# Sixteen slots of h at multiples of 256 bytes, and the shifted half of a weight buffer in one of its turns out of four

## The chip, the core and the metric

The kernel runs on one core of a Trainium2 chip. The metric is device time in microseconds (us) of one execution. The median of three runs of the kernel before is 1770.55 us (1770.16 to 1771.66).

## What is computed

One macaron block of a Conformer: a half-step SwiGLU feed-forward, a token mixer (attention heads beside multi-scale pooling groups), a second half-step feed-forward, and a final RMSNorm. Each of the three normalised inputs is scaled and shifted by numbers that depend on a conditioning vector `c`. Cut to what matters here:

```python
mod = silu(c) @ w_ada + b_ada                         # 9 sections of 2048, "ada" below
h = modulate(rmsnorm(x, g1), sh1, sc1)
x = x + 0.5 * gate1 * swiglu(h, ffn1_w_in, ffn1_w_out)
h = modulate(rmsnorm(x, g2), sh2, sc2)
x = x + gate2 * mixer(h, w_in, ..., w_out)
h = modulate(rmsnorm(x, g3), sh3, sc3)
x = x + 0.5 * gate3 * swiglu(h, ffn2_w_in, ffn2_w_out)
return rmsnorm(x, final_norm_g)
```

There are 256 tokens, 2048 channels and 5504 hidden channels, all in float32.

## The kernel before

**Arithmetic.** Each float32 operand of the large products is split into a high part, rounded to the TensorE type `fp32r`, and a low part, the remainder. A product takes three matmuls, high by high, low by high and high by low (`mm3`, L242, L243, L244). So a 128x128 weight tile costs three matmuls, each with 256 moving columns (the tokens) and one weight load.

**Weights.** The weights come in 614 pieces of eight tiles (128x1024 float32, 512 KB), in the order in which TensorE will use them. `next_piece` brings a piece into use and at the same time starts work for the next ones: ScalarE casts a piece to `wh` in two halves (L193), VectorE subtracts to make `wl` in two halves (L203), and SyncE's queue loads a raw piece (L185). Four `wh` buffers and three `wl` buffers go round in turn (`part_tile`), and five raw buffers. Beside this run 144 loads of `ada` (1 MB each), each with a multiplication on VectorE (L112) that yields 128 numbers of `mod`; they are spread over the pieces at fixed rates, so how many there are for each piece doesn't depend on how fast anything runs.

**Activations.** The moving operand of the products is one of: `h` (L242 to L244, 16 tiles per normalised input, tag `h`, 16 slots), `hraw` (the same slots, 258 columns, made before the root of the norm is known), `g` and `mix` (tag `pair`, 43 slots of 2048 bytes), and in the q, k and v projections (`project`, L768) the weights themselves, where `h` is the stationary operand. Each tile of these holds the high part and behind it the low part.

**Addresses.** They decide this change; all here are bytes within a partition, in the built program. The slots of `h` begin at 29440, which is a multiple of 256. A slot is as long as the largest tile of its tag, `hraw` with 2 x 272 columns, which is 2176 bytes, eight and a half times 256. So slots 0, 2, 4, ... begin at a multiple of 256, and slots 1, 3, 5, ... 128 past one. In the first feed-forward the tiles of channel blocks 0 to 15 lie in slots 1 to 8, 11, 10, 15, 14, 13, 9, 12 and 0, so that blocks 0 to 11 alternate between the two, 12 and 13 lie 128 past a multiple, and 14 and 15 at one. The high and the low part are 1024 bytes apart in `h` and in `g`. All 43 slots of `g` and `mix` begin at multiples of 256. A small tile (`gap`, 16 columns) puts all `wh` buffers, two `wl` buffers and the raw buffers 64 past a multiple of 256, and the last `wl` buffer lies 192 past one. The fourth `wh` buffer is 32 columns longer (`BEHIND`), and its second half begins 16 columns, 64 bytes, later than it otherwise would, so that these four weight tiles lie 128 past a multiple of 256. Below, 64, 128 and 192 stand for these distances, and 0 for a multiple of 256.

```python
GAP = 16
BEHIND = {"wh": (0, 0, 0, 2 * GAP), "wl": (0, 0, 0)}
```

Of the kernel before, what the change touches and what calls it, by code (L numbers as in the profile page):

```python
# [10 lines left out]
F32 = mybir.dt.float32  # L11
F32R = mybir.dt.float32r
# [4 lines left out]
P = 128  # L17
SEQ = 256
# [5 lines left out]
HD = 128  # L24
UT = 8
UN = UT * P
# [21 lines left out]
NEG = -3.0e38  # L48
GAP = 16
BEHIND = {"wh": (0, 0, 0, 2 * GAP), "wl": (0, 0, 0)}  # L50
WARM = 9
QSCALE = float(HD) ** -0.5

# [12 lines left out]
def block_kernel(ctx, tc, order, xT, cvec, wada, wts, wf, vecs, out):  # L66
# [105 lines left out]
    HALF = UN // 2  # L172

    def part_tile(kind):

        behind = BEHIND[kind]
        i = turns[kind] % len(behind)
        turns[kind] += 1
        w = wpool.tile([P, UN + behind[i]], F32R, tag=f"{kind}{i}", name=kind, bufs=1)
        return w[:, :HALF], w[:, HALF + behind[i] // 2 : UN + behind[i] // 2]  # L180

    def load_piece():
        if state["loaded"] < wts.shape[0]:
# [76 lines left out]
    class Stats:  # L260
# [6 lines left out]
        def add(self, d):  # L267
            t = {}

            def square():  # L270
                t["sq"] = work.tile([P, SEQ], F32, tag="act", name="sq", bufs=3)
                nc.scalar.activation(t["sq"], x[d], AF.Square)

            def total():
                if d == KD - 1:
                    self.last = t["sq"]
                elif self.acc is None:
                    self.acc = work.tile([P, SEQ], F32, tag="gf", name="acc", bufs=3)
                    nc.vector.tensor_copy(out=self.acc, in_=t["sq"])
                else:  # L280
                    nc.vector.tensor_add(out=self.acc, in0=self.acc, in1=t["sq"])

            later(square, total)
            if d == KD - 1:
                step_chains(0)

        def rms_row(self, meanwhile=None, between=None):

            st = sm_tile()
            parts = self.parts or (self.acc, self.last)  # L290
            for i, part in enumerate(parts):
                nc.tensor.matmul(st[:, :SEQ], lhsT=ones, rhs=part, start=i == 0, stop=i == len(parts) - 1)  # L292
            self.row = work.tile([P, SEQ], F32, tag="rrow", name="rrow", bufs=1)
            guess, rest = (work.tile([P, SEQ], F32, tag="hu", name=n, bufs=3) for n in ("guess", "rest"))
            first, newton = inverse_root(self.row, st[:, :SEQ], D, guess, rest)
            first()
            if between:
                between()
            newton()
            if meanwhile:  # L300
                meanwhile()
            return self.row

    def make_h(d, rrow, a_col, b_col):

        u = work.tile([P, SEQ], F32, tag="hu", name="hu", bufs=3)
        nc.vector.scalar_tensor_tensor(out=u, in0=x[d], scalar=a_col, in1=rrow, op0=ALU.mult, op1=ALU.mult)
        h = big.tile([P, 2, SEQ], F32R, tag="h", name="h", bufs=16)

        def high():  # L310
            nc.scalar.activation(h[:, 0, :], u, AF.Identity, bias=b_col)  # L311

        def low():
            nc.vector.scalar_tensor_tensor(  # L314
                out=h[:, 1, :], in0=u, scalar=b_col, in1=h[:, 0, :].bitcast(F32), op0=ALU.add, op1=ALU.subtract
            )

        return h, high, low

    def make_raw(d, a_col, b_col):  # L320

        h = big.tile([P, 2, SEQ + 16], F32R, tag="h", name="hraw", bufs=16)[:, :, : SEQ + 2]
        b2 = b_col.to_broadcast([P, 2])

        def high():
            nc.scalar.activation(h[:, 0, :SEQ], x[d], AF.Copy, scale=a_col)
            nc.scalar.copy(out=h[:, 0, SEQ:], in_=b2)

        def low():
            nc.vector.scalar_tensor_tensor(  # L330
                out=h[:, 1, :SEQ], in0=x[d], scalar=a_col, in1=h[:, 0, :SEQ].bitcast(F32),
                op0=ALU.mult, op1=ALU.subtract,
            )
            nc.vector.tensor_sub(out=h[:, 1, SEQ:], in0=b2, in1=h[:, 0, SEQ:].bitcast(F32))

        return h, high, low
# [40 lines left out]
    def swiglu(ab, j, g):  # L377

        t = {}

        def act():
            t["s"] = work.tile([P, SEQ], F32, tag="act", name="silu", bufs=3)
            nc.scalar.activation(t["s"], ab[:, :SEQ], AF.Silu)

        def product():
            t["g"] = work.tile([P, SEQ], F32, tag="gf", name="gf", bufs=3)
            nc.vector.tensor_mul(out=t["g"], in0=ab[:, SEQ:512], in1=t["s"])
            g[j] = pair_tile([P, 2, SEQ], F32R, f"g{j}")

        def high():  # L390
            nc.scalar.copy(out=g[j][:, 0, :], in_=t["g"])

        def low():
            nc.vector.tensor_sub(out=g[j][:, 1, :], in0=t["g"], in1=g[j][:, 0, :].bitcast(F32))

        return act, product, high, low
# [377 lines left out]
    def norm_heads(pts, name):  # L774
# [4 lines left out]
        def squares(tt):  # L779
            nc.scalar.copy(out=qr[tt], in_=pts[tt].rearrange("p (a b) -> p a b", a=4))  # L780
            for i in range(4):
                junk = work.tile([P, HD], F32, tag="act", name="junk", bufs=3)
                nc.scalar.activation(
                    junk, qr[tt][:, i, :], AF.Square, accum_out=ss[:, tt * 4 + i : tt * 4 + i + 1]
                )
# [309 lines left out]
```

## Time and profile before

| | |
|---|---|
| median of the runs | 1770.55 us |
| the profiled execution: its time, its span | 1770.31 us, 1768.6 us |
| TensorE matmul busy | 1753.8 us (99%), 14,966 matmuls |
| TensorE granted clock | 0.998 of full speed |
| VectorE busy | 1371.4 us (78%) |
| ScalarE busy | 922.2 us (52%) |
| DMA, mean over the span | 272 GB/s |

A busy share says little of TensorE, since the records of matmuls that follow each other overlap: one takes 277 to 280 ns in the record, but the next starts some 115 ns after it. What counts is the distance between starts, which the timeline gives, and the number of matmuls in a window. Times in the views are counted from the start of the span.

### The profile page before, as it was taken

The page shows a single profiled execution, that of the slowest core. Times are in us where ns is not written, and L with a number is a line of the kernel's source. Part 1 is how long each engine was busy: PE and PEld are TensorE (multiplying, and loading weights), DVE is VectorE, ACT ScalarE, POOL GpSimd, SP SyncE. Part 2 cuts the span into 40 slices and gives each one's busy share as a digit, 9 for nine tenths or more (in the row PEclk, how much of TensorE's full clock was granted, in tenths as well). Part 3 has the DMA queues.
Part 4 walks back from the last instruction along what each step waited for, and adds up shares of the span by engine and source line. Part 5 has one row for each costly group of instructions (what it writes and reads, how often), then busy time and mean ns, then how long its engine had stood idle before and what let it go on. Part 6 is the DMA issues. An engine that isn't in the chain of part 4 may idle for free.

```text
span 1768.6 us, 37313 instructions
## 1 busy us (share of the span) xinstructions
PE 1753.8 (99%) x14966; PEld 1743.8 (99%) x14966; DVE 1371.4 (78%) x2390; ACT 922.2 (52%) x1871; POOL 8.3 (0%) x54
## 2 busy tenths in 40 slices
PE   9999999999999999999999999999999999999997
PEld 7999999999999999999999999999999999999997
DVE  7899889999988888797989998777765555555554
ACT  7644445555554444477766555544444444544442
POOL 0000000000000000100000000000000000000000
PEclk9999999999999999999999999999999999999999
DMA  9889898888889989767966977877775555555553
GB/s 367 317 319 331 319 339 316 309 308 314 311 319 335 328 329 334 286 237 301 344 223 248 330 285 249 296 268 259 262 258 189 189 188 191 191 191 192 194 195 112
DMA packets 111937, 480.79 MB, mean 272 GB/s; under 512 B 12425, under 2 KB 12689, under 8 KB 93329
## 3 DMA queue, kind: packets, MB, share of 16 engines
q1 hardware_dynamic: 111762, 478.39, 75.4%
q8 instruction: 117, 1.92, 0.4%
q14 instruction: 58, 0.48, 0.1%
HBM read 476.24 MB, written 2.11 MB: 270 GB/s over the span
## 4 chain that ended last, share of the span: by engine, by line
PE 98%; ACT 1%; DMA 1%; DVE 0%; issue 0%; SPq 0%; DVEq 0%
PE mm L243 30%; PE mm L242 29%; PE mm L244 29%; PE mm L768 8%; DMA ada<-in_wada 1%; ACT wh L193 0%; ACT spill L454 0%; DVE y L1029 0%; PE sm L802 0%; PE sm L832 0%; PE sm L881 0%; PE sm L872 0%; PE sm L292 0%; PE sm L699 0%; PE sm L701 0%
## 5 line engine op out<-in xcount | busy, mean ns | idle before, releaser
L193 ACT CAST wh<-raw 128x512 fp32r<-128x512 f32 x1228 | 701.2, 620 | 725.1 <-PE mm L243 442.0
L203 DVE TENSOR_TENSOR wl<-raw,wh 128x512 fp32r<-128x512 f32 x1228 | 788.2, 686 | 319.0 <-issue 285.2
L242 PE MATMUL mm<-h,wh 128*128 128x256 f32 x2800 | 782.1, 279 | 0.8 <-ACT h L311 0.4
L243 PE MATMUL mm<-h,wh 128*128 128x256 f32 x2800 | 782.8, 280 | 0.1
L244 PE MATMUL mm<-h,wl 128*128 128x256 f32 x2800 | 781.9, 279 | 0.0
L242 PEld LDWEIGHTS mm<-h,wh 128*128 128x128 f32 x2800 | 526.3, 188 | 2.0 <-ACT spill L454 1.0
L243 PEld LDWEIGHTS mm<-h,wh 128*128 128x128 f32 x2800 | 525.8, 188 | 0.4 <-DVE h L314 0.3
L244 PEld LDWEIGHTS mm<-h,wl 128*128 128x128 f32 x2800 | 526.0, 188 | 0.0
L244 PE MATMUL mm<-g,wl 128*128 128x256 f32 x1376 | 380.8, 277 | 0.0
L243 PE MATMUL mm<-g,wh 128*128 128x256 f32 x1376 | 380.5, 277 | 0.0
L242 PE MATMUL mm<-g,wh 128*128 128x256 f32 x1376 | 380.5, 276 | 0.0
L112 DVE SCALAR_TENSOR_TENSOR ada<-ada,crow 128x2048 f32<-128x2048 f32 x144 | 329.2, 2286 | 23.5 <-DMA ada<-in_wada 22.9
L243 PEld LDWEIGHTS mm<-g,wh 128*128 128x128 f32 x1376 | 258.4, 188 | 0.0
L244 PEld LDWEIGHTS mm<-g,wl 128*128 128x128 f32 x1376 | 258.4, 188 | 0.0
L242 PEld LDWEIGHTS mm<-g,wh 128*128 128x128 f32 x1376 | 258.3, 188 | 0.0
L768 PE MATMUL mm<-wh,h 128*128 128x256 f32 x768 | 137.3, 282 | 0.0
L768 PEld LDWEIGHTS mm<-wh,h 128*128 128x128 f32 x768 | 117.4, 188 | 0.5 <-issue 0.2
L768 PE MATMUL mm<-wl,h 128*128 128x256 f32 x384 | 107.2, 279 | 0.0
L768 PEld LDWEIGHTS mm<-wl,h 128*128 128x128 f32 x384 | 72.3, 188 | 0.0
L244 PE MATMUL mm<-mix,wl 128*128 128x256 f32 x256 | 70.9, 277 | 0.0
L243 PE MATMUL mm<-mix,wh 128*128 128x256 f32 x256 | 70.8, 277 | 0.0
L242 PE MATMUL mm<-mix,wh 128*128 128x256 f32 x256 | 70.8, 277 | 0.0
(166 smaller groups left out, 1002.9 us busy)
## 6 DMA issues: line engine op xcount, KB each, us to landing
raw<-in_wts SPq DMA_DIRECT2D x614, 512.0 KB, 4.4
ada<-in_wada SPq DMA_DIRECT2D x144, 1024.0 KB, 7.6
x<-in_xT SPq DMA_DIRECT2D x4, 512.0 KB, 5.5
out<-y SPq DMA_DIRECT2D x8, 256.0 KB, 2.2
fb<-frow_d SPq DMA_DIRECT2D x4, 256.0 KB, 8.0
vec<-in_vecs SPq DMA_DIRECT2D x1, 109.5 KB, 10.1
wfc<-in_wf SPq DMA_DIRECT2D x1, 64.0 KB, 5.7
crow<-in_cvec SPq DMA_DIRECT2D x1, 8.0 KB
```

The costliest lines, as they stand in the source:

```text
L112: nc.vector.scalar_tensor_tensor(out=r, in0=r, scalar=1.0, in1=crow, op0=ALU.mult, op1=ALU.mult, accum_out=mod[section][:, t : t + 1],)
L193: nc.scalar.copy(out=wh[i], in_=raws[0][:, i * HALF : (i + 1) * HALF])
L203: nc.vector.tensor_sub(out=wl[i], in0=raw[:, i * HALF : (i + 1) * HALF], in1=wh[i].bitcast(F32))
L242: nc.tensor.matmul(out_ap, lhsT=wh, rhs=hk[:, 0, :], start=start, stop=False, skip_group_check=shared)
L243: nc.tensor.matmul(out_ap, lhsT=wh, rhs=hk[:, 1, :], start=False, stop=False, skip_group_check=shared)
L244: nc.tensor.matmul(out_ap, lhsT=wl, rhs=hk[:, 0, :], start=False, stop=stop, skip_group_check=shared)
L768: nc.tensor.matmul(pts[tt][:, c], lhsT=lhs, rhs=rhs[:, c], start=k == 0 and not half and not i, stop=k == KD - 1 and i == 2, skip_group_ch ...
```

## The change

Four edits. `h` and `hraw` get slots of 576 columns (2304 bytes, nine times 256), so that all 16 slots begin at a multiple of 256; the two parts of `h` stay 1024 bytes apart, and the low part of `hraw` moves to 1152 bytes behind the high one (from 1088). The second half of the fourth `wh` buffer is shifted only where the turn of that buffer is 1 modulo 4; in its other turns it lies 64 past a multiple of 256, like every other `wh` half. To pay for the 2048 bytes, the tags `hu` and `act` get two buffers in place of three. The rest of the tiles move up by 2048 bytes, so their distances from multiples of 256 stay as they were.

```diff
+SLOT = 576
...
         behind = BEHIND[kind]
         i = turns[kind] % len(behind)
+        turn = turns[kind] // len(behind)
         turns[kind] += 1
         w = wpool.tile([P, UN + behind[i]], F32R, tag=f"{kind}{i}", name=kind, bufs=1)
-        return w[:, :HALF], w[:, HALF + behind[i] // 2 : UN + behind[i] // 2]
+        at = HALF + (behind[i] // 2 if turn % 4 == 1 else 0)
+        return w[:, :HALF], w[:, at : at + HALF]
...
-                t["sq"] = work.tile([P, SEQ], F32, tag="act", name="sq", bufs=3)
+                t["sq"] = work.tile([P, SEQ], F32, tag="act", name="sq", bufs=2)
...
-            guess, rest = (work.tile([P, SEQ], F32, tag="hu", name=n, bufs=3) for n in ("guess", "rest"))
+            guess, rest = (work.tile([P, SEQ], F32, tag="hu", name=n, bufs=2) for n in ("guess", "rest"))
...
+    def h_slot(name, half):
+
+        return big.tile([P, SLOT], F32R, tag="h", name=name, bufs=16)[:, : 2 * half].rearrange("p (a b) -> p a b", a=2)
+
...
-        u = work.tile([P, SEQ], F32, tag="hu", name="hu", bufs=3)
+        u = work.tile([P, SEQ], F32, tag="hu", name="hu", bufs=2)
...
-        h = big.tile([P, 2, SEQ], F32R, tag="h", name="h", bufs=16)
+        h = h_slot("h", SEQ)
...
-        h = big.tile([P, 2, SEQ + 16], F32R, tag="h", name="hraw", bufs=16)[:, :, : SEQ + 2]
+        h = h_slot("hraw", SEQ + P // 4)[:, :, : SEQ + 2]
...
-            t["s"] = work.tile([P, SEQ], F32, tag="act", name="silu", bufs=3)
+            t["s"] = work.tile([P, SEQ], F32, tag="act", name="silu", bufs=2)
...
-                junk = work.tile([P, HD], F32, tag="act", name="junk", bufs=3)
+                junk = work.tile([P, HD], F32, tag="act", name="junk", bufs=2)
```

On every engine the instructions stand in the same order before and after. On TensorE these rows of before stand 293 us into the span, in the first feed-forward; `h_2883` and `h_3061` are the tiles of blocks 14 and 15 (slots 12 and 0), `h_977` and `h_1165` those of blocks 4 and 5 (slots 5 and 6), and `wh_3693` and `wl_3735` lie at 64.

```order
L242 MATMUL mm_3799<-h_2883,wh_3693 128x256
L243 MATMUL mm_3799<-h_2883,wh_3693 128x256
L244 MATMUL mm_3799<-h_2883,wl_3735 128x256
L242 MATMUL mm_3799<-h_3061,wh_3693 128x256
L243 MATMUL mm_3799<-h_3061,wh_3693 128x256
L244 MATMUL mm_3799<-h_3061,wl_3735 128x256
L242 MATMUL mm_3828<-h_977,wh_3693 128x256
L243 MATMUL mm_3828<-h_977,wh_3693 128x256
L244 MATMUL mm_3828<-h_977,wl_3735 128x256
L242 MATMUL mm_3828<-h_1165,wh_3693 128x256
L243 MATMUL mm_3828<-h_1165,wh_3693 128x256
L244 MATMUL mm_3828<-h_1165,wl_3735 128x256
```

The same rows stand there after the change, and only the slots differ: `h_977`, 128 past a multiple of 256 before, now begins at one.

On VectorE the only rows that differ carry a wait. Here stand the first tiles of the mixer's h (`hu` is the product of x, scale and norm, from which `h` is made); before:

```order
L307 SCALAR_TENSOR_TENSOR hu_9847<-x0_74,a4_103,rrow_9777 128x256
L307 SCALAR_TENSOR_TENSOR hu_9860<-x0_74,a4_103,rrow_9777 128x256
L314 SCALAR_TENSOR_TENSOR h_9849<-hu_9847,b4_106,h_9849 128x256 [waits Activation_49]
L307 SCALAR_TENSOR_TENSOR hu_9871<-x0_74,a4_103,rrow_9777 128x256
L314 SCALAR_TENSOR_TENSOR h_9862<-hu_9860,b4_106,h_9862 128x256 [waits Activation_49]
```

and after:

```order
L314 SCALAR_TENSOR_TENSOR hu_9847<-x0_74,a4_103,rrow_9777 128x256
L314 SCALAR_TENSOR_TENSOR hu_9860<-x0_74,a4_103,rrow_9777 128x256
L321 SCALAR_TENSOR_TENSOR h_9849<-hu_9847,b4_106,h_9849 128x256 [waits Activation_49]
L314 SCALAR_TENSOR_TENSOR hu_9871<-x0_74,a4_103,rrow_9777 128x256 [waits DVE_49]
L321 SCALAR_TENSOR_TENSOR h_9862<-hu_9860,b4_106,h_9862 128x256 [waits Activation_49]
```

Nothing moved; the third `hu` now waits for VectorE's own earlier instruction, since it takes the buffer of the first. Four rows of VectorE and 28 of ScalarE differ in this way, each by a wait of an engine for itself, and none on the other engines.

## Rows read from the trace of the kernel before

**Rows 1.** The page: busy time by engine, and the chain that ended last.

```profile
PE 1753.8 (99%) x14966; PEld 1743.8 (99%) x14966; DVE 1371.4 (78%) x2390; ACT 922.2 (52%) x1871; POOL 8.3 (0%) x54
PE 98%; ACT 1%; DMA 1%; DVE 0%; issue 0%; SPq 0%; DVEq 0%
```

**Rows 2.** Windows of five stages: PE, PEld, DVE, ACT, POOL busy, clock, DMA.

```profile
40.00:500.00 460.00, 460.00 (x3931) 460.00 (x3931) 421.12 (x693) 232.11 (x446) 0.00 (x0) 1.00 0.89 319
505.00:739.00 234.00, 234.00 (x2055) 234.00 (x2055) 196.87 (x337) 113.38 (x223) 6.94 (x42) 1.00 0.91 331
752.00:905.00 153.00, 153.00 (x1297) 151.81 (x1297) 133.74 (x255) 110.97 (x288) 0.34 (x3) 1.00 0.79 292
1060.00:1520.00 460.00, 460.00 (x3939) 460.00 (x3939) 300.82 (x496) 223.97 (x434) 0.00 (x0) 1.00 0.66 233
1522.00:1740.00 218.00, 218.00 (x1915) 218.00 (x1915) 116.48 (x205) 104.36 (x192) 0.00 (x0) 1.00 0.57 193
```

**Rows 3.** Timeline of PE, first feed-forward: start us, duration us, instruction.

```profile
292.77 0.28 PE L242 MATMUL mm<-h,wh 128*128 128x256 f32 x1
...
294.47 0.28 PE L242 MATMUL mm<-h,wh 128*128 128x256 f32 x1
...
296.57 0.28 PE L242 MATMUL mm<-h,wh 128*128 128x256 f32 x1
```

**Rows 4.** The same view, first matmuls of the first output product.

```profile
504.70 0.28 PE L244 MATMUL mm<-g,wl 128*128 128x256 f32 x1
...
507.52 0.28 PE L244 MATMUL mm<-g,wl 128*128 128x256 f32 x1
...
507.88 0.28 PE L244 MATMUL mm<-g,wl 128*128 128x256 f32 x1
...
508.21 0.28 PE L244 MATMUL mm<-g,wl 128*128 128x256 f32 x1
```

**Rows 5.** The same view around one shifted half, in the same product.

```profile
590.34 0.28 PE L242 MATMUL mm<-g,wh 128*128 128x256 f32 x1
...
590.69 0.28 PE L242 MATMUL mm<-g,wh 128*128 128x256 f32 x1
...
592.11 0.28 PE L242 MATMUL mm<-g,wh 128*128 128x256 f32 x1
```

**Rows 6.** Groups by line and form: count, busy us, mean ns, idle before.

```profile
L242 PE MATMUL mm<-h,wh 128*128 128x256 f32 x2800 | 782.1, 279 | 0.8 <-ACT h L311 0.4 <-ACT spill L454 0.3
L242 PE MATMUL mm<-g,wh 128*128 128x256 f32 x1376 | 380.5, 276 | 0.0
L242 PE MATMUL mm<-mix,wh 128*128 128x256 f32 x256 | 70.8, 277 | 0.0
```

**Rows 7.** Timeline of PE in the projections, two stretches.

```profile
753.70 0.39 PE L768 MATMUL mm<-wh,h 128*128 128x256 f32 x2
...
755.06 0.39 PE L768 MATMUL mm<-wh,h 128*128 128x256 f32 x2
...
759.32 0.40 PE L768 MATMUL mm<-wh,h 128*128 128x256 f32 x2
...
760.73 0.28 PE L768 MATMUL mm<-wh,h 128*128 128x256 f32 x1
```

**Rows 8.** Waits from 184 to 244 us: us in total, times, longest.

```profile
DVE ada L112 <- DMA ada<-in_wada: 6.8, 5, 2.2
```

**Rows 9.** The window of the same stretch, columns as in rows 2.

```profile
184.00:244.00 60.00, 60.00 (x514) 60.00 (x513) 54.70 (x95) 26.91 (x49) 0.00 (x0) 1.00 0.90 331
```

**Rows 10.** Timeline of DVE, subtractions at two places (starts 0.60 us apart).

```profile
177.58 2.49 DVE L203 TENSOR_TENSOR wl<-raw,wh 128x512 fp32r<-128x512 f32 x4
...
228.28 1.88 DVE L203 TENSOR_TENSOR wl<-raw,wh 128x512 fp32r<-128x512 f32 x3
```

**Rows 11.** Timeline of PE, the first matmuls that read these.

```profile
184.34 0.28 PE L244 MATMUL mm<-h,wl 128*128 128x256 f32 x1
...
229.43 0.28 PE L244 MATMUL mm<-h,wl 128*128 128x256 f32 x1
```

## Prediction

> **What bounds the kernel now.** The page first: TensorE is busy 99% of the span, and 98% of the chain that ended last is PE [rows 1]. The kernel is thus as long as its 14,966 matmuls are apart, plus a few us at both ends, as long as nothing comes late. A duration says nothing here, so next the windows, for matmuls per stage [rows 2]. A window counts those that reach over its edges as well, some 2.4 more than start in it (0.28 us over 0.117). In the first feed-forward's input product, with h as moving operand, that is 460 us / 3,929 = 117.1 ns from start to start, in the second's 460 / 3,937 = 116.9; in the output products, with g, 234 / 2,053 = 114.0 and 218 / 1,913 = 114.0. The reader should see that this does not follow the load on the other engines: VectorE is busy 92% of the window at 40 us, 65% in that at 1060 us and 84% in that at 505 us, and DMA 0.89, 0.66 and 0.91, and the two h stages are alike, as are the two of g. The clock is 1.00 in all of them, the upper level (2.4 GHz).
>
> Then the timeline inside a stage of h [rows 3]. From 292.77 to 294.47 us TensorE reads blocks 14 and 15, both at 0: 15 matmuls in 1.70 us, 113.3 ns each. At 294.47 it goes on to block 4, at 128, and alternates from there: 18 matmuls in 2.10 us, 116.7 ns. Same code, same weights at 64, same neighbours. In the g stage, where every moving tile lies at 0, a steady stretch has 113.3 as well, and the three matmuls before 590.69 take 0.35 us; the twelve after it, of a shifted half, take 1.42 us, 118 ns each [rows 5]. So there are two things that cost: a moving operand at 128, and weights at 128.
>
> There is a third, and it is what makes me doubt. The rate has a memory. At the entry from h to g, 24 matmuls from 504.70 to 507.52 take 117.5 ns each, though moving tiles lie at 0 and weights at 64; it ends where the piece of the `wl` buffer at 192 comes, and from 507.88 three matmuls take 0.33 us [rows 4]. In the projections the same pair of distances (h at 0, weights at 64) runs at 113.3 ns from 753.70 and at 117.5 from 759.32, twelve matmuls each [rows 7]. So the slow rate, once entered, can outlast its cause until a distance changes.
>
> **The change, part by part.** The sum is made against the profiled execution's own 1770.3 us, which is 0.2 us under the median.
>
> Slots of h. The h groups of L242, L243 and L244 have 2,800 matmuls each, 8,400 [rows 6]. The first 130 or so belong to the start, where pieces come late. With all slots at 0 the other 8,270 should run as blocks 14 and 15 do now: from 117.0 (the mean of the two h windows) to 113.3, 3.65 ns each, -30.2 us. Both ends: nothing, if they run slow all the time; -30.2 if always as in [rows 3]. I take the fast end, since the nearest case, the g stages, has just these distances throughout and is at 114.0 with its shifted halves included.
>
> Shifted halves that stay. One piece in 16 keeps one, 24 matmuls a piece: 8,270 / 384 = 22 of them among h. One costs twelve times 118 less 113.3, some 0.06 to 0.07 us with the matmul behind it: +1.5 us.
>
> Shifted halves that go, in g and mix. 3 x (1,376 + 256) = 4,896 matmuls [rows 6] are 204 pieces with 51 shifted halves, 13 after: 38 x 0.07 = -2.7 us.
>
> `hraw` and the projections. The 240 matmuls with hraw keep a low part at 128 and gain at most the same 3.65 ns, 0.9 us; I take -0.5. In the 1,152 of L768 h is the stationary operand and the weights move; both rates occur there with h at either distance, so the bounds are all slow and all fast, +1.4 and -3.5 us about what is now a mixture; I take -0.5 for the shifted halves that go.
>
> Two buffers in place of three. The new waits are of VectorE and ScalarE for themselves, 32 in all; one bounds at an instruction's length, under 0.7 us (the `wl` subtraction is the longest of the neighbours, [rows 10]), the other at nothing, since the earlier reader stands ahead in the same queue. What covers them is the lead of `wl` over TensorE, up to 4.9 us (below). Zero.
>
> What comes due next. A faster TensorE asks for pieces sooner, and VectorE is nearly full in the first feed-forward. Look at its lead. The third of the four subtractions from 177.58 ends at 177.58 + 2 x 0.60 + 0.69 = 179.47 and is read at 184.34, 4.87 us ahead. The first of the three from 228.28 ends at 228.97 and is read at 229.43, 0.46 us ahead [rows 10, 11]. In between VectorE worked 54.7 of 60 us and waited 6.8 for ada loads, so it was full [rows 8, 9]. After the change TensorE is 16 pieces x 24 x 3.65 ns = 1.4 us earlier at that point: the lead would be 0.9 below zero, and TensorE waits as long. If loads land no sooner, the five late ada products add up to 3 pieces x 24 x 3.65 ns = 0.26 us each. +2 us, between 0.9 and 5 (a lead as short as this at several other places of the stage, each 1 us more).
>
> Sum: 1770.3 - 30.2 + 1.5 - 2.7 - 0.5 - 0.5 + 2 = 1739.9; I add 0.6 for entries into stages that run slow for up to two pieces (48 x 4.2 ns = 0.2 us each, three of them): 1740.5 us.
>
> A rule speaks against all of this. The Trainium skill's page "SBUF — State Buffer", section "Who interferes with whom", gives TensorE two independent read ports, one for the moving operand and one for the weight load, and says: "PE and ACT never wait on anyone." By it distances in SBUF would be worth nothing and the time stay at 1770.3. [Rows 3] disagree: the one thing that changes at 294.47 is which slots are read.
>
> **The rivals.** *The slow rate sticks* (the other side). If what keeps the pipeline fast today is that it is disturbed every four pieces, then with a disturbance every sixteen and with no change of slot distance it may sit at 117.5. For it: [rows 4, 7]. Against: in g the fast rate holds from one shifted half to the next and through the changes from `wl` at 64 to 192 and back; and the one slow stretch ended at such a change, which comes in every third piece, shifted half or not. Each slow matmul costs 4.2 ns, and there are 8,270 + 4,896 that could be: the gain of 30 us is gone when 7,100 of these 13,170, 54%, run slow, and with all of them slow the time is 1740.5 + 13,170 x 4.2 ns = 1796 us. Partly, with the slow rate held from a disturbance to the next `wl` at 192 in a third of the pieces, it is 1740.5 + 18 = 1759.
>
> *VectorE or DMA becomes the bound.* DMA is at 0.91 and 331 GB/s where it is asked most [rows 2, 9]; TensorE would ask for 3% more, 341 GB/s. If the whole first stage ran as fast as it does now, the change would keep only the second's gain: 3,930 x 3.8 ns = 15 us lost, 1755. Against it: the g stage has the same rates of loads, moves 331 GB/s at 114.0 ns and shows no wait of TensorE; I give it up to 1750.
>
> *The distance is not the cause.* If h is slow for what goes with it (copies to spill tiles, additions), only the shifted halves change: 38 fewer in g and mix and 64 fewer in h, at 0.02 to 0.07 us each, 1764 to 1768. For it there is only the rule above; against it [rows 3], in one stage within 4 us.
>
> **How the numbers follow.** The forecast, 1734 to 1748 us, 0.74. Slow rate in part, 1748 to 1765, 0.09; sticking for most, above 1765, 0.07. First stage bound by VectorE or DMA, 1746 to 1755, 0.06. Distance not the cause, 1764 to 1768, 0.04. The range for 8 in 10 takes in the forecast, with the stalls at their bound, and the half of the partial cases: 1734 to 1756. A measurement of this kernel tells 0.2%, 3.5 us, from no change. Faster by more: the first two, the fourth and a part of the last, 0.90; within it 0.04; slower 0.06.
>
> **What would show it.** Right: the windows at 40 and 1060 us hold 3.0% more matmuls, at 113.5 to 113.8 ns, like those of g; twelve slow matmuls in one piece out of 16; VectorE's share in the first stage rises by 3%, with waits for ada there longer, and TensorE waits for `wl` near 230 us for about 1 us at a time. Wrong: steady stretches of h at 117.5 with weights at 64, above all such that last past a `wl` at 192; or a first feed-forward that is no shorter while the second is.

## The result, and the profile after

The changed kernel takes 1745.68 us (median of 4 runs, 1745.34 to 1746.95), against 1770.40 for the kernel before beside it (1770.16 to 1771.66). The ratio is 0.986 [0.9843, 0.9877], so it is faster by 24.7 us. The profiled execution took 1745.73 us with a span of 1744.0.

The page of the kernel after; its lines answer to [rows 1]:

```profile
PE 1726.4 (99%) x14966; PEld 1714.9 (98%) x14966; DVE 1369.9 (79%) x2390; ACT 923.7 (53%) x1871; POOL 8.3 (0%) x54
PE 95%; DMA 2%; DVE 2%; ACT 1%; issue 0%; SPq 0%; DVEq 0%
```

The counts are the same and TensorE is still the chain, but DMA and VectorE now hold 4% of it, where they had 1%. The windows of the kernel after, columns as in [rows 2] (the one at 505 us now reaches past the end of g, so that g itself is read from the table below):

```profile
40.00:500.00 460.00, 457.24 (x4016) 456.20 (x4016) 427.24 (x706) 239.43 (x456) 0.00 (x0) 1.00 0.91 325
752.00:905.00 153.00, 153.00 (x1287) 151.88 (x1286) 133.13 (x251) 108.98 (x286) 0.45 (x4) 1.00 0.78 286
1060.00:1520.00 460.00, 460.00 (x4056) 460.00 (x4055) 305.43 (x505) 229.49 (x444) 0.00 (x0) 1.00 0.68 237
```

In the second feed-forward the window holds 4,056 matmuls in place of 3,939, so 460 us / 4,053.6 = 113.5 ns each. The first holds 4,016 in place of 3,931, which is 114.6 ns; here TensorE is no longer busy all the time (457.24 of 460). The window over the projections holds 1,287 against 1,297, but it no longer covers the same matmuls, since the stage now starts 11 us earlier (741.7 us in place of 752.3); the table below has the projections themselves. The clock is 1.00 in all three, as before, so none of this is the clock.

The timeline of TensorE in the kernel after, at five places; start, duration, instruction. The first three rows are the same matmuls as in [rows 3], the next two those of [rows 4], then the place in g that was a shifted half, then four of the projections:

```profile
289.60 0.28 PE L245 MATMUL mm<-h,wh 128*128 128x256 f32 x1
...
291.30 0.28 PE L245 MATMUL mm<-h,wh 128*128 128x256 f32 x1
...
293.34 0.28 PE L245 MATMUL mm<-h,wh 128*128 128x256 f32 x1
...
495.15 0.28 PE L247 MATMUL mm<-g,wl 128*128 128x256 f32 x1
...
497.87 0.28 PE L247 MATMUL mm<-g,wl 128*128 128x256 f32 x1
...
580.71 0.28 PE L245 MATMUL mm<-g,wh 128*128 128x256 f32 x1
...
582.07 0.28 PE L245 MATMUL mm<-g,wh 128*128 128x256 f32 x1
...
743.09 0.40 PE L775 MATMUL mm<-wh,h 128*128 128x256 f32 x2
...
744.50 0.40 PE L775 MATMUL mm<-wh,h 128*128 128x256 f32 x2
...
748.78 0.40 PE L775 MATMUL mm<-wh,h 128*128 128x256 f32 x2
...
750.20 0.40 PE L775 MATMUL mm<-wh,h 128*128 128x256 f32 x2
```

From 289.60 to 291.30 the 15 matmuls of blocks 14 and 15 take 1.70 us as before; the 18 behind them, of blocks 4 to 9, now take 2.04 us, 113.3 ns each as well (2.10 before). The entry into g, 24 matmuls from 495.15 to 497.87, takes 113.3 ns each; it was 117.5. At 580.71 the twelve matmuls that were a shifted half in [rows 5], and now lie at 64, take 1.36 us, 113.3 each. In the projections it went the other way: the stretch that ran at 113.3 in [rows 7] takes 1.41 us for twelve, 117.5 each, like the other.

The waits of the kernel after from 40 to 500 us, in total, times and longest:

```profile
DVE ada L113 <- DMA ada<-in_wada: 24.1, 27, 1.9
...
PE mm L247 <- DVE wl L206: 2.8, 5, 0.9
```

and one of the five, in the timeline of TensorE (in brackets the idle time ahead and its releaser):

```profile
212.19 0.28 PE L246 MATMUL mm<-h,wh 128*128 128x256 f32 x1
213.38 0.39 PE L247 MATMUL mm<-h,wl 128*128 128x256 f32 x1 [0.91 <-DVE wl L206]
213.60 0.28 PE L245 MATMUL mm<-h,wh 128*128 128x256 f32 x1
```

VectorE waits 24.1 us for `ada` loads in this stretch, twice the 11.9 of before, and five times TensorE waits for a `wl` that VectorE makes behind such a wait. At 213.38 the matmul starts 1.19 us after the one ahead of it.

The table below adds up the distances from each matmul's start to the next one's, from the traces, by the stage that the matmul belongs to, for this kernel and the experiments. "Of it waits" sums what each distance of over 130 ns in the first feed-forward's h has beyond 130 ns; it is a part of the column ahead. There are 4,128 matmuls with h in the first feed-forward, 4,272 in the second and the mixer, 4,128 with g and 1,152 in the projections.

| us | h, first | of it waits | h, the rest | g | projections |
|---|---|---|---|---|---|
| before | 485.2 | 1.8 | 499.6 | 470.5 | 136.6 |
| after | 475.4 | 6.2 | 485.5 | 468.4 | 137.9 |
| slots alone | 479.6 | 8.4 | 487.4 | 470.4 | 138.2 |
| fewer shifts alone | 485.3 | 3.2 | 498.4 | 468.4 | 135.9 |
| never shifted | 476.4 | 7.8 | 484.9 | 467.8 | 137.7 |
| no distance changes, a short execution | 475.8 | 6.8 | 484.9 | 467.8 | 138.0 |
| the same kernel, a long execution | 488.1 | 1.9 | 484.9 | 477.0 | 138.0 |
| h at 128 | 479.8 | 5.4 | 491.6 | 468.8 | 137.2 |
| h in two groups | 485.9 | 5.3 | 498.8 | 468.7 | 136.8 |
| mixer's h alternates | 475.2 | 6.0 | 486.4 | 468.4 | 137.2 |
| lag of four | 471.0 | 2.0 | 485.4 | 468.4 | 139.2 |
| half product | 471.0 | 2.1 | 485.4 | 468.4 | 137.9 |
| lag of four, never shifted | 470.3 | 2.2 | 484.7 | 467.8 | 139.3 |
| before with two buffers | 488.1 | 4.7 | 499.6 | 470.5 | 137.0 |

### The profile page after: what moved, and what is told of

Its sections match the earlier page's. It is cut to its first block, busy times and chain, and to the rows that moved or that the text cites. A ratio compares the mean times of both kernels' runs of the same rounds, so it can differ in the third digit from the quotient of the medians.

```text
span 1744.0 us, 37330 instructions
## 1 busy us (share of the span) xinstructions
PE 1726.4 (99%) x14966; PEld 1714.9 (98%) x14966; DVE 1369.9 (79%) x2390; ACT 923.7 (53%) x1871; POOL 8.3 (0%) x54
## 4 chain that ended last, share of the span: by engine, by line
PE 95%; DMA 2%; DVE 2%; ACT 1%; issue 0%; SPq 0%; DVEq 0%
PE mm L247 29%; PE mm L245 29%; PE mm L246 28%; PE mm L775 8%; DMA ada<-in_wada 2%; DVE wl L206 1%; DVE ada L113 0%; ACT wh L196 0%; ACT spill L461 0%; DVE y L1036 0%; PE sm L888 0%; PE sm L809 0%; PE sm L839 0%; PE sm L295 0%; PE sm L879 0%
## 5 line engine op out<-in xcount | busy, mean ns | idle before, releaser
L247 PE MATMUL mm<-h,wl 128*128 128x256 f32 x2800 | 774.1, 276 | 2.8 <-DVE wl L206 2.8
L245 PE MATMUL mm<-h,wh 128*128 128x256 f32 x2800 | 774.3, 277 | 0.7 <-ACT spill L461 0.5
L246 PE MATMUL mm<-h,wh 128*128 128x256 f32 x2800 | 773.4, 276 | 0.1
L113 DVE SCALAR_TENSOR_TENSOR ada<-ada,crow 128x2048 f32<-128x2048 f32 x144 | 329.4, 2287 | 48.4 <-DMA ada<-in_wada 47.8
L775 PEld LDWEIGHTS mm<-wh,h 128*128 128x128 f32 x768 | 117.6, 188 | 0.5 <-issue 0.2
```

Source lines behind the costliest of these rows:

```text
L113: nc.vector.scalar_tensor_tensor(out=r, in0=r, scalar=1.0, in1=crow, op0=ALU.mult, op1=ALU.mult, accum_out=mod[section][:, t : t + 1],)
L245: nc.tensor.matmul(out_ap, lhsT=wh, rhs=hk[:, 0, :], start=start, stop=False, skip_group_check=shared)
L246: nc.tensor.matmul(out_ap, lhsT=wh, rhs=hk[:, 1, :], start=False, stop=False, skip_group_check=shared)
L247: nc.tensor.matmul(out_ap, lhsT=wl, rhs=hk[:, 0, :], start=False, stop=stop, skip_group_check=shared)
L775: nc.tensor.matmul(pts[tt][:, c], lhsT=lhs, rhs=rhs[:, c], start=k == 0 and not half and not i, stop=k == KD - 1 and i == 2, skip_group_ch ...
```

## The experiments

The theory of the prediction is that the distances of the operands from multiples of 256 bytes set whether matmuls start 113.3 or about 117.8 ns apart. The rivals are that the slow rate sticks, that something other than h's distance makes h slow, and that VectorE or DMA takes the gain. Diffs are against the changed kernel unless the text says otherwise. Where no range is given, a time is the median of a kernel's runs.

### The two parts, each alone

The slots alone, with the shift in every turn of the fourth `wh` buffer:

```diff
-        at = HALF + (behind[i] // 2 if turn % 4 == 1 else 0)
+        at = HALF + behind[i] // 2
```

> Only the slots of h (and the two buffers that pay for them); the half of the fourth wh buffer is shifted in every turn, as before. If the rate follows from the distances (theory one): steady stretches of h at 113.3 ns, twelve slow matmuls in every fourth piece, 115 more of them at 2.2 ns over 24 matmuls, 0.053 us each, so about 6 us more than the changed kernel, less up to 1.5 us in the projections if the more frequent shift ends slow stretches there: 1750 us. If the slow rate is kept off by the shifts (theory two): 1745 or less.

Measured: 1754.47 us (1751.37 to 1758.27), ratio 0.99 [0.9882, 0.9918].

The shift alone, in the kernel before, with its slots and its three buffers:

```diff
+        turn = turns[kind] // len(behind)
...
-        return w[:, :HALF], w[:, HALF + behind[i] // 2 : UN + behind[i] // 2]
+        at = HALF + (behind[i] // 2 if turn % 4 == 1 else 0)
+        return w[:, :HALF], w[:, at : at + HALF]
```

> Only the shift in one turn of four; slots of h and three buffers as before. Theory one: the g and mix stages lose 38 shifted halves, 2.3 us; h keeps its alternation at 116.7 ns and gains at most 1 us: 1767 to 1769. If the shift and not the slots made the gain: 1750 or less. If a rarer shift lets the slow rate stick: over 1771.

Measured: 1766.58 us (1764.70 to 1766.85), ratio 0.9966 [0.9953, 0.9979].

Beside them the kernel before took 1771.44. So the slots are worth 17.0 us with the shift in every turn, the rarer shift 4.9 us with the old slots, and both together 24.7. By the medians they do more together than apart, though the runs of the slots alone lie up to 6.9 us from each other. The table shows where: h falls by 17.8 us with the slots, by 1.1 with the rarer shift and by 23.9 with both. Of the 6.1 us between the slots alone and both, 2.2 are waits, which the slots alone raise to 8.4 us. Among h tiles that alternate a shifted half more or less changes little (the h of the first feed-forward is the same 485 us with either), while among tiles that all lie at 0 it costs. That the slots alone move 5.6 us of h in the first stage and 12.2 in the rest, with g as before, rules out that something other than the slots' distance makes h slow (the two buffers, which come with the slots, gain nothing by themselves: last experiment).

### Is the shift needed at all?

The fourth `wh` buffer keeps its extra columns, so that the last `wl` buffer stays at 192, but its half is never shifted:

```diff
-        at = HALF + (behind[i] // 2 if turn % 4 == 1 else 0)
+        at = HALF
```

> The changed kernel with no half ever shifted; the last wl buffer stays at 192, so one distance still changes in every third piece. Theory one: 38 shifted halves fewer at 0.053 us, 2 us: 1743.7, with the projections as slow as they are. Theory two (the shift ends slow stretches): slow pieces at 117.7 ns in h or g after the entries into stages, each 0.1 us, and 1746 or more.

Measured: 1745.75 us (1743.55 to 1747.04), ratio 0.985 [0.9834, 0.9866]; the changed kernel has 0.986 [0.9843, 0.9877], so the two can't be told apart. Every column of the table but one gains a little (0.6 us in h of the rest, 0.6 in g, 0.2 in the projections); the first feed-forward is 1.0 us longer, since its waits grow by 1.6.

Then the last distance that changes in the steady stretches, the `wl` buffer at 192, is taken away as well, by 32 columns behind the last `wl` buffer in place of the fourth `wh` buffer. All weights now lie at 64 and all of h and g at 0:

```diff
-BEHIND = {"wh": (0, 0, 0, 2 * GAP), "wl": (0, 0, 0)}
+BEHIND = {"wh": (0, 0, 0, 0), "wl": (0, 0, 2 * GAP)}
...
-        at = HALF + (behind[i] // 2 if turn % 4 == 1 else 0)
+        at = HALF
```

> No half shifted, and the last wl buffer at 64 as well (the 32 columns stand behind it), so that no distance changes within a stage of h or g. Theory one without memory: 1743.7 as without the shift. With the memory that the projections show: the rate with which a stage is entered stays to its end; the second h stage is entered from hraw, at 120 ns, and would stay at 117.7 for its 4,000 matmuls, 17 us more, and the g stage behind it another 8: 1760 to 1770. If the change of wl to 192 costs something itself, less than 1743.

Measured: ten runs in two groups, seven from 1743.91 to 1749.30 and three from 1765.12 to 1768.22. The median is 1746.23 us, the ratio 0.9887 [0.985, 0.9925]; neither says much of two groups. The profiled execution was one of the short ones, and its stages are those of the kernel that is never shifted. So it was run once more, on another chip, to find a long one in a trace:

> The kernel with all wl buffers at 64 and no shift once more, to see where its long executions (three of ten, 20 us over the others) lose the time. If the slow rate is kept through a whole stage, an execution is near 1745, or a stage of h or g runs at 117.8 ns throughout with all clocks and loads as before: near 1766. If the long ones are something else: times between, or slower stretches with late loads.

Measured: eight runs, four from 1742.77 to 1748.81 and four from 1761.94 to 1767.71 (median 1755.37, ratio 0.9902 [0.9858, 0.9946]). The profiled execution took 1766.93. Its windows:

```profile
40.00:500.00 460.00, 460.00 (x3908) 460.00 (x3908) 418.38 (x687) 231.26 (x443) 0.00 (x0) 1.00 0.89 317
505.00:735.00 230.00, 230.00 (x1955) 230.00 (x1954) 191.43 (x327) 108.02 (x212) 0.00 (x0) 1.00 0.89 321
...
1060.00:1520.00 460.00, 460.00 (x4057) 460.00 (x4057) 312.24 (x524) 232.33 (x451) 0.00 (x0) 1.00 0.69 238
```

and the same windows of the short execution of the same kernel:

```profile
40.00:500.00 460.00, 456.96 (x4012) 455.71 (x4012) 427.43 (x707) 237.66 (x457) 0.00 (x0) 1.00 0.90 324
505.00:735.00 230.00, 230.00 (x2025) 229.89 (x2024) 193.25 (x331) 109.43 (x217) 6.94 (x42) 1.00 0.92 331
...
1060.00:1520.00 460.00, 460.00 (x4061) 460.00 (x4060) 306.12 (x505) 230.02 (x445) 0.00 (x0) 1.00 0.68 237
```

In the long one the first feed-forward runs at 460 / 3,905.6 = 117.8 ns, through h and g alike, with TensorE busy all the time: of its 258 pieces all but the second and the third have 117.6 to 118.0 ns. From the mixer on both run at 113.3. The clock is 1.00 in both, TensorE waits less in the long one, and no address differs. So the same operands at the same distances have two rates, and a run can stay in the slow one for 700 us when nothing disturbs it.

One thing that changes the rate can be seen in the short execution: a wait of TensorE can do it, with no distance changed. Here are the rows at two waits for `wl` in its first feed-forward, with every weight at 64 and every tile of h at 0:

```profile
183.08 0.28 PE L246 MATMUL mm<-h,wh 128*128 128x256 f32 x1
184.53 0.38 PE L247 MATMUL mm<-h,wl 128*128 128x256 f32 x1 [1.17 <-DVE wl L206]
184.75 0.28 PE L245 MATMUL mm<-h,wh 128*128 128x256 f32 x1
...
198.65 0.28 PE L246 MATMUL mm<-h,wh 128*128 128x256 f32 x1
198.84 0.39 PE L247 MATMUL mm<-h,wl 128*128 128x256 f32 x1
199.07 0.28 PE L245 MATMUL mm<-h,wh 128*128 128x256 f32 x1
...
212.35 0.28 PE L245 MATMUL mm<-h,wh 128*128 128x256 f32 x1
```

The 118 matmuls ahead of the first wait start 113.5 ns apart. The 118 from 184.75 to 198.65 take 13.90 us, 117.8 each. Behind the second wait, which makes one distance 196 ns long, the 117 from 199.07 to 212.35 take 13.28 us, 113.5 each. Not every wait does this: of the eight in this stage from 120 us on, one brings the slow rate and the next ends it. At the start, up to 36 us, pieces come late in both executions. The short one leaves the last of these waits at the fast rate; the long one leaves it at the slow rate and then has no distance of over 130 ns in h and g until the mixer. So the two groups of times are probably a matter of the rate at which such waits are left; two traces can't show that it is always so.

With the `wl` at 192 in place, such a stretch is short. In the trace of the slots alone a wait starts one in the same way, and it ends with the first matmuls of the next piece whose `wl` lies at 192 (127.15 is the first of them):

```profile
124.22 0.38 PE L247 MATMUL mm<-h,wl 128*128 128x256 f32 x1 [0.63 <-DVE wl L206]
124.44 0.28 PE L245 MATMUL mm<-h,wh 128*128 128x256 f32 x1
...
127.15 0.28 PE L247 MATMUL mm<-h,wl 128*128 128x256 f32 x1
...
127.62 0.28 PE L245 MATMUL mm<-h,wh 128*128 128x256 f32 x1
...
129.66 0.28 PE L245 MATMUL mm<-h,wh 128*128 128x256 f32 x1
```

From 124.44 to 127.15 the 23 matmuls take 2.71 us, 117.8 each; from 127.62 to 129.66 the 18 take 2.04 us, 113.3 each.

Of 18 runs without the `wl` at 192, seven are long; of 20 runs with it and with slots at 0 (the changed kernel, the one never shifted and the three of the section on waits below), none is above 1747.04. Eight of the 20 have no shifted half either. (The slots alone, with their many shifted halves, are not counted.)

### Distance, or change of distance?

All tiles of h, each in a slot of the same size, but 128 bytes into it:

```diff
-        return big.tile([P, SLOT], F32R, tag="h", name=name, bufs=16)[:, : 2 * half].rearrange("p (a b) -> p a b", a=2)
+        return big.tile([P, SLOT], F32R, tag="h", name=name, bufs=16)[:, 32 : 32 + 2 * half].rearrange("p (a b) -> p a b", a=2)
...
-        h = h_slot("hraw", SEQ + P // 4)[:, :, : SEQ + 2]
+        h = h_slot("hraw", SEQ + 16)[:, :, : SEQ + 2]
```

> All 16 slots of h at 128 past a multiple of 256, the same for every tile (hraw too, low part 64 further). If a moving operand at 128 is itself what costs (theory one): steady stretches of h at 117.7 ns, 8,400 x 4.2 ns = 35 us more than the changed kernel, less the stalls of the first stage that go: 1772 to 1778, over the kernel before. If the change of distance from tile to tile was what cost before: 1745, as with all slots at 0.

Measured: 1756.24 us (1755.52 to 1758.36), ratio 0.9915 [0.9901, 0.993], which is neither. Two windows of its first feed-forward:

```profile
89.00:130.00 41.00, 41.00 (x349) 41.00 (x349) 39.22 (x66) 17.42 (x32) 0.00 (x0) 1.00 0.90 311
134.50:157.50 23.00, 23.00 (x205) 22.87 (x203) 19.56 (x34) 10.40 (x19) 0.00 (x0) 1.00 0.90 333
```

The first is 41 us / 346.6 = 118.3 ns, the second 23 / 202.6 = 113.5, with the same distances in both. Piece by piece, with pieces counted from 0, 112 of the first feed-forward's 172 with h run at 113.3 to 114.3 ns and 51 at 117 or more; in the second it is 111 and 48 of 166. Seven slow stretches start from pieces 23, 71, 119, 167, 407, 455 and 503, those in which a shifted half and the `wl` at 192 meet, every 48 pieces. Five of them end 16 pieces later, at the next shifted half; that of 71 ends at piece 80, that of 167 in g. The `wl` at 192 that comes in every third piece between ends none of the five; such pieces run at 118.9 there. It does end slow stretches that a wait of TensorE has started: behind waits in pieces 49 and 69 the matmuls are 117.8 ns apart, and 113.3 again from the first matmuls of the `wl` at 192 in pieces 50 and 71; the end in piece 80, too, follows a wait, of 1.36 us in piece 79. So what ends the slow rate depends on how it was entered. A tile at 128 is thus not slow by itself.

The changes between tiles, then. Blocks 0 to 7 at 0 and 8 to 15 at 128, which makes 0.95 changes of h's distance inside a piece of 24 matmuls (mean of pieces 60 to 169), where the kernel before has 5.25; with those from one piece to the next it is 1.12 and 6.13:

```diff
-    def h_slot(name, half):
+    def h_slot(name, half, at=0):
...
-        return big.tile([P, SLOT], F32R, tag="h", name=name, bufs=16)[:, : 2 * half].rearrange("p (a b) -> p a b", a=2)
+        return big.tile([P, SLOT], F32R, tag="h", name=name, bufs=16)[:, at : at + 2 * half].rearrange("p (a b) -> p a b", a=2)
...
-        h = h_slot("h", SEQ)
+        h = h_slot("h", SEQ, 32 * (d // 8))
```

> The changed kernel, but the tiles of channel blocks 8 to 15 lie at 128 and those of blocks 0 to 7 at 0: as many tiles at 128 as in the kernel before, but the distance changes twice in 16 blocks and not at nearly every block. If each change of distance costs (the theory after the run with all of h at 128): 2 changes in 48 matmuls against some 14 before, at about 10 ns for the three matmuls behind one, 3.5 us over 8,400 matmuls, and some stretches that stay slow at 128: 1749 to 1758. If tiles at 128 are read slower beside ones at 0: as before, 1765 or more.

Measured: 1768.02 us (1766.56 to 1777.02), ratio 0.9984 [0.9972, 0.9995]. That each change costs a fixed price is wrong: a fifth of the changes costs what all of them did (the shift alone, with the old slots, has 485.3 and 498.4 us of h in the table, this kernel 485.9 and 498.8). The windows:

```profile
40.00:110.00 70.00, 69.84 (x615) 69.65 (x614) 62.76 (x103) 42.13 (x78) 0.00 (x0) 1.00 0.90 322
250.00:480.00 230.00, 230.00 (x1956) 230.00 (x1955) 211.99 (x351) 118.85 (x239) 0.00 (x0) 1.00 0.87 312
```

In the first only blocks below 8 are read (the others come in from 148 us on), and it runs at 70 / 612.6 = 114.3 ns. Once both groups are read in turn it is 230 / 1,953.6 = 117.7. Of the pieces 100 to 171, 30 have no change of h's distance between their matmuls, and in 29 of these at least 23 of the 24 matmuls take more than 116 ns. So a change can put TensorE into the slow rate, and it stays there for matmuls that change nothing.

The time is the one that the other theory gave (tiles at 128 slower beside tiles at 0: 1765 or more), and the trace bears it out in part. All of these 30 pieces lie at 128. In the second feed-forward the tiles at 128 take 118.1 ns on the mean and those at 0 115.3; in the kernel before it is 117.9 and 115.8. The place alone does not do it: the first 18 matmuls of piece 104, at 128 behind a shifted half, run at 113.3. The difference is in what ends the slow rate that a change has brought. Pieces wholly at 0 with the `wl` at 192 are back at 113.3 in their second half (22 pieces of the second feed-forward); those wholly at 128 with the same `wl` take 118.6 there (21 pieces).

### The projections

They became slower, and the suspicion was that h at two distances in turn is what ended slow stretches there. The mixer's h alone goes to 0 and 128 in turn:

```diff
-        h = h_slot("h", SEQ)
+        h = h_slot("h", SEQ, 32 * (d % 2) if rrow is rows.get(2) else 0)
```

> The changed kernel, but the mixer's 16 tiles of h lie at 0 and 128 in turn, as all did before; there they are the stationary operand in the projections and the moving one in six pool tiles. If the projections stick at 117.8 ns because no distance of the stationary operand changes (theory: a change ends the slow rate): the projections fall by 1 to 2 us from 137.9, the pool tiles rise by about 1: 1744.5 to 1746. If they are slow for another reason: projections at 138, total 1747.

Measured: 1747.19 us (1745.60 to 1748.65), ratio 0.9865 [0.9849, 0.9882]. The projections come down by 0.7 us of the 1.3 that they had lost, and the mixer's other products, which read the same h as moving operand, take 0.9 more. It is no gain. The kernels agree on the sign: with h alternating or in groups the projections take 135.9 to 137.2 us (137.2 also with all of it at 128), with h at 0 and the same lag 137.7 to 138.2.

### The waits of the first feed-forward

If late `ada` loads hold up VectorE, and `wl` behind them, then later use of the loads should end it. In the changed kernel the product follows three pieces behind its load; here it is four:

```diff
-LAG0, LAG = 1, 3
+LAG0, LAG = 1, 4
```

> The changed kernel, each ada product one piece later (four pieces after its load, not three). If TensorE's stalls in the first feed-forward (6.2 us in the changed kernel against 1.8 before) come of ada loads that land after VectorE wants them: waits of VectorE for ada fall from 24 us to under 8, stalls to 2 or 3, 1742. If the raw loads land too late as well, or VectorE's work alone fills it: stalls of 5 or more, 1745.

Measured: 1742.67 us (1742.34 to 1742.81), ratio 0.9837 [0.9822, 0.9851]. The window of its first feed-forward, and the group of all its `ada` products (busy us, mean ns, idle ahead and its releaser):

```profile
40.00:500.00 460.00, 460.00 (x4055) 460.00 (x4054) 434.23 (x716) 241.89 (x464) 0.00 (x0) 1.00 0.89 327
```

```profile
L113 DVE SCALAR_TENSOR_TENSOR ada<-ada,crow 128x2048 f32<-128x2048 f32 x144 | 329.0, 2284 | 1.6 <-DMA ada<-in_wada 1.5
```

The group's waits for loads are 1.5 us in the whole kernel, where the changed one has 47.8; the first feed-forward now runs at 460 / 4,052.6 = 113.5 ns, like the second. This uses VectorE more (434 of 460 us), not less, so VectorE's amount of work was not the limit; the place of the wait was. The projections take 1.3 us more, in waits, so 3.0 of 4.4 us remain.

The other way round, less work behind each wait: this kernel leaves out half of each `ada` product (channels 1024 to 2047 of the sum) and loads what the changed one loads.

```diff
-                out=r, in0=r, scalar=1.0, in1=crow, op0=ALU.mult, op1=ALU.mult,
+                out=r[:, : D // 2], in0=r[:, : D // 2], scalar=1.0, in1=crow[:, : D // 2], op0=ALU.mult, op1=ALU.mult,
```

> Leaves out half of each ada product (1024 of 2048 columns); loads and order as in the changed kernel. VectorE has 144 x 1.07 us less to do. If VectorE's work fills it in the first feed-forward and the ada waits only add to that: stalls there fall from 6.2 to below 3 us and the time to 1741 or 1742, with the waits for ada still there. If the loads bound the stage (raw pieces land too late): stalls of 5 us or more, 1745.

Measured: 1739.76 us (1739.58 to 1740.19), ratio 0.9821 [0.9806, 0.9835]. The same group, and the window of the first feed-forward:

```profile
L113 DVE SCALAR_TENSOR_TENSOR ada<-ada,crow 128x1024 f32<-128x1024 f32 x144 | 175.6, 1220 | 10.2 <-DMA ada<-in_wada 9.5
```

```profile
40.00:500.00 460.00, 460.00 (x4056) 460.00 (x4055) 378.63 (x717) 239.49 (x462) 0.00 (x0) 1.00 0.89 328
```

Here too the waits in the first feed-forward fall from 6.2 to 2.1 us, and the stage is the same 471.0 us as with a lag of four. DMA moves as much as in the changed kernel (328 GB/s from 40 to 500 us, against 325), so DMA as such was no bound either. The waits for `ada` fall as well, from 47.8 to 9.5 us, which was not expected, so this run alone does not part the work from the waits; the lag of four does.

The two findings together, a lag of four and no shifted half:

```diff
-LAG0, LAG = 1, 3
+LAG0, LAG = 1, 4
...
-        at = HALF + (behind[i] // 2 if turn % 4 == 1 else 0)
+        at = HALF
```

> The version that the runs point to: the changed kernel with ada products one piece later and no half shifted (the last wl buffer stays at 192). If both gains add: 1742.7 less 2 us of shifted halves, 1740.5 to 1741.5. If without the shift the slow rate stays longer after entries into stages: 1743 or more.

Measured: 1740.27 us (1740.13 to 1740.46), ratio 0.9822 [0.9807, 0.9837]. It is the best kernel of the study that computes everything, 5.4 us under the changed one.

### Two buffers in place of three

In the kernel before, `act` and `hu` get two buffers, and nothing else changes:

```diff
-        u = work.tile([P, SEQ], F32, tag="hu", name="hu", bufs=3)
+        u = work.tile([P, SEQ], F32, tag="hu", name="hu", bufs=2)
...
-            t["s"] = work.tile([P, SEQ], F32, tag="act", name="silu", bufs=3)
+            t["s"] = work.tile([P, SEQ], F32, tag="act", name="silu", bufs=2)
```

(and likewise at the other places of the two tags)

> The kernel before with two buffers in place of three under act and hu, and nothing else. My step: the 32 waits of VectorE and ScalarE for themselves cost nothing that TensorE sees: within 1 us of the kernel before in each stage, 1770 to 1772. If they delay the subtractions: more stalls in the first feed-forward than the 1.8 us of before, over 1773.

Measured: 1772.63 us (1771.07 to 1775.47, ten runs) against 1771.76 of the kernel before (19 runs), ratio 1.0005 [0.9996, 1.0015]. No cost is shown, and one of up to 2.7 us (0.15%) is not excluded. The profiled execution, at 1774.87 one of the longer ones, has 4.7 us of waits in the first feed-forward, where the one of before has 1.8, so a part of the waits there may come from the buffers; this stays open.

## Why the prediction was right, and where it was off

The time was forecast as 1740.5 us and is 1745.7; the profiled executions are 24.6 us apart where the sum had 29.8.

**Slots of h: right, to the size.** The steady part of h went from 117.0 to 113.3 ns, as the term said. From the table, h as a whole went from 984.8 to 960.9 us, and without the waits (1.8 before, 6.2 after) by 28.3 us; the prediction had 30.2 less 1.5 for the shifted halves that stay less 0.6 for entries, 28.1. The part on its own gives 17.0 with a shifted half in every fourth piece.

**Shifted halves: right, a little smaller.** A piece with one runs at 115.5 ns, twelve of its matmuls at 117.7 (118 in the forecast), so it costs 24 x 2.2 = 0.053 us; where it meets the `wl` at 192 it costs 0.073, and the mean in g is 0.060, the low end of the 0.06 to 0.07 of the forecast. In g and mix they gave 2.5 us of the 2.7 forecast, 0.1 of it at the first entry into g.

**What comes due next: the mechanism right, the size not.** `wl` late behind `ada` loads was named, near 230 us, about 1 us at a time; there are five such waits, at 122.9, 197.5, 212.2, 227.1 and 241.3 us, with 0.4 to 1.2 us from one start to the next. The term was +2 in bounds of 0.9 to 5, and it measured +4.4. The lag of four and the half product both remove it, each by another end of the same chain. VectorE's share rose by 1.5% (421.1 to 427.2 us of the window) rather than 3%; with the loads in time, in the lag of four, it is 434.2 us, 3.1%.

**Projections and `hraw`: wrong in sign.** "I take -0.5" for each; the projections lost 1.3 us, which is nearly the bound given for all slow (+1.4), and `hraw` gained nothing (29.3 us in both traces). In the projections 46 of 48 pieces now run above 116.5 ns, where 28 did before (means without distances of over 130 ns). Here the rival "the slow rate sticks" came true. These two and the waits make 1.8 + 0.6 + 2.4 = 4.8 of the 5.2 us by which the sum missed.

**The reason itself: half wrong.** "So there are two things that cost: a moving operand at 128, and weights at 128" does not hold for the first: h at 128 throughout runs at 113.3 in most pieces. What [rows 3] showed, block 4 at 128 following block 15 at 0, was the beginning of a stretch that changes distance, not of one at a bad distance. The third thing, that the rate has a memory, is the main one: h in two groups shows that a fifth of the changes is enough to keep it slow, and the kernel without any change shows that it can be slow with none, behind a wait. Still, beside tiles at 0 it is the tiles at 128 that lose most (117.9 ns against 115.8 before), and in the trace of the two groups the `wl` at 192 ends the slow rate at 0 and not at 128. The remedy was right because slots at one distance take the changes away, and would have worked at 1756 us, though less well, at 128.

**The sticking rival** was given 0.16 and did not come in h and g. The reason given against it, that the `wl` at 192 ends a slow stretch, is borne out at h = 0: without that buffer 7 of 18 runs took 1762 to 1768 us where the others took 1743 to 1749, and with it none did; and the trace of the slots alone shows it end one. It does not hold at h = 128 for the stretches that a shifted half or a change of distance starts. So the forecast depended on a detail that the change left alone, and on slots at 0 and not at 128. The first was seen beforehand, in one stretch; the second was chosen for a reason that holds only in part, and there the forecast had luck.

**VectorE or DMA as the bound** took part of the first stage (the waits above), not its gain. **The distance is not the cause** was refuted by the slots alone.

The Trainium skill's page "SBUF — State Buffer", section "Who interferes with whom", says that TensorE never waits on anyone at SBUF's ports. The traces agree in so far as the load of the other engines and of DMA does not set the rate. They do not agree if it is taken to say that where the operands lie is free: 3.7 ns of 117 in a matmul of h, on the mean, hang on it.

Not settled: what in the chip has the two rates, why one wait changes the rate and the next does not, and why the projections, with h as the stationary operand, hold the slow one past a `wl` at 192.

## What to carry to other kernels

When matmuls follow each other without waits, compare the distances between their starts in like stretches; two sharp values at the same clock mean that something about the operands or about what ran ahead decides, and slots that all begin at the same distance from a multiple of 256 bytes are cheap to try. A rate with a memory has to be judged by many runs, since one profile may show the lucky case, and a small regular disturbance (here one weight buffer at another distance) can be what keeps the times together, while a single wait can change the rate. And where the bound becomes faster, look for the producer with the least lead and for what it waits in front of it: here one constant, a lag of four pieces in place of three, was worth 3 us.

## What the runs showed of the hardware that was not expected

- Matmuls of 256 fp32r columns, each with a weight load, start 113.3 or 117.8 ns apart at the same clock (1.00, the upper level, 2.4 GHz) in stretches in which h or g lies at 0 and all weights at 64, and both occur with the same distances: 117.8 and 113.3 in two executions of one kernel over the same 460 us (3,908 and 4,012 matmuls, the latter with 3 us of waits).
- A wait of TensorE can turn one rate into the other with no distance changed: 113.5, 117.8 and 113.5 ns in three stretches of 117 or 118 matmuls, parted by distances of 1.45 us and of 0.20 us.
- What ends the slow rate depends on where the moving operand lies and on how the rate was entered. With h at 0 it lasted only in the kernel without the `wl` at 192. With h at 128, stretches begun by a shifted half outlast that buffer (118.9 ns in its pieces) and end at a shifted half in five of seven; two that a wait began ended at that buffer.
- Changes of distance don't add up: 0.95 inside a piece of 24 matmuls cost as much as 5.25 (h at 984.7 and 983.7 us).
